# The second output projection of a two-layer encoder, begun for all row tiles in the last recurrent head

## The chip, the cores and the metric

The kernel runs on one NeuronCore of a Trainium2 chip. The time is device time in microseconds (us) of one execution. The kernel before takes 2702.19 us (median of three runs, 2701.62 to 2704.5).

The engines, by the names used below: TensorE (PE: matmuls; PEld: loads of the stationary operand, which overlap them), VectorE (DVE), ScalarE (ACT), GpSimd (POOL) and SyncE (SP), which here issues most DMAs. Each engine works through its own instructions in a fixed order.

## The reference, cut to what matters

Two layers over 1024 tokens of width 1024 (all float32). Layer 0 mixes tokens by windowed attention, layer 1 by a bidirectional gated recurrence (HGRN2) of 8 heads; each mixer also has 4 cross-attention heads of width 128 into 256 memory tokens. Both groups share one input and one output projection, and each layer ends with a convolutional feed-forward part.

```python
for layer in range(DEPTH):
    u = rmsnorm(h, norm_g[layer, 0])
    mem_kv = mem_n @ w_mem_kv[layer]
    if kind == 0:
        y = mixer_window_attn(u, mem_kv, ...)
    elif kind == 1:
        y = mixer_hgrn2(u, mem_kv, ...)
    h = h + rmsnorm(y, norm_g[layer, 1])
    f = conv_ffn(rmsnorm(h, norm_g[layer, 2]), ...)
    h = h + rmsnorm(f, norm_g[layer, 3])

def mixer_hgrn2(u, mem_kv, w_in, lb_fwd, lb_bwd, norm_g, w_out):
    q, i, zf, zb, gate, xq = jnp.split(u @ w_in, ...)
    ...
    o = gla_chunked(q, k_f, v, lf_f) + flip_t(gla_chunked(flip_t(q), flip_t(k_b), flip_t(v), flip_t(lf_b)))
    o = rmsnorm(o, ...) * jax.nn.silu(gate)
    return jnp.concatenate([o, memory_cross_attn(xq, mem_kv)], axis=-1) @ w_out
```

The last line is the output projection that the change is about: its input has 8 x 128 columns of recurrent heads and 4 x 128 of cross heads, 12 blocks of 128; its output has 1024 columns.

## The kernel before

*Precision.* Every float32 product of the projections is made of three matmuls (`mm3`, lines 80 to 83): each operand is split into a high part, a copy rounded to the type `float32r` (ScalarE), and a low part, the remainder (VectorE). `split` (line 85) does this for activations, `wunit` (line 69) for weights: it reads a unit of 128 x 1024 from DRAM into a staging buffer and writes a pair `wh`, `wl` into a ring of 4 pairs, or `xwh`, `xwl` into a pool that is handed to it.

*Tiles.* Tokens are cut into 8 row tiles of 128, or two blocks of 512 (b = 0, 1). The normalised rows `u` are kept transposed and split in `uh`, `ul`, of 8 blocks of 128 features by 1024 tokens.

*Order of work.* Pieces are written out in program order; a scheduler that works with a model of the engines turns this order into priorities and fixes each engine's order: an instruction further on is taken ahead where an engine would be free in the model and the instruction's inputs are there. `tc.high_priority` lifts single pieces. On the chip each engine follows the fixed order and waits on semaphores.

*The recurrence* (`hgrn`, from line 939). For each head, `proj` (line 1044) makes q, the two gates' inputs f and b (block by block, `proj_fm`), and for pairs of heads v and the output gate (`proj_tm`), in the order of the strings `ORD` (line 38); those of head h + 1 stand behind head h. For head 7 the order is `q0 f0 q1 b1`, and f1 and b0 only after its first and second direction. V and G (line 945) hold v and the gate of three heads in turn (slot h mod 3). `head` (line 1224) runs `direction` for (d, b) = (0,0), (1,1), (0,1), (1,0): a chain of VectorE, ScalarE and GpSimd operations (a scan at line 1091, products of decays, `ER` at line 1155), block products on TensorE (`pa`), transposes (line 1165) and state updates (`pu`, line 1170; `S`, line 1179). Then `output` (line 1182) runs for b = 1 and b = 0: products `po`, sums of squares, scaling, transposes, and `ot`, which goes by SP's queue to `oT[1][h]` in DRAM (line 1207). The products of the projections go through two PSUM banks `pj`.

*The cross units* (`cross_unit`, line 185) each make one block of one cross head: a query projection from `uh`, `ul`, scores, softmax, transposes, products, and `xo`, stored to `oT[1][8 + h]` by ScalarE's queue. `xo` shares its one buffer with `ot`. A new cross head first loads weights and its keys and values (`cross_head`, line 178), through an `E` buffer of the directions. `HX` (line 35) says how many units stand behind each of a head's four directions and two outputs: heads 2, 4, 6 have two (behind the third and fourth direction), head 7 has two (behind the second and third).

*The output projection of layer 1* (`WOut`, line 371; `wo1`). It runs over the two column halves of the weights, 12 blocks of 128 rows of weights in 6 units each, tiles in the order 4, 5, 6, 7, 0, 1, 2, 3. `early` (line 381), called behind head 7's third direction, begins tiles 4 and 5 in the two `pj` banks with heads 0 to 5 and cross heads 0 and 1. `open` (line 394), behind the fourth, adds the other two cross heads to these two. `finish` (line 465) makes the first half for all tiles: each group of blocks is read from `oT`, split (`operands`, `rows_of`), multiplied; heads 6 and 7 come last. It keeps the first half in `y0`. The second half reads and splits all 12 blocks again, per tile; then follow the norm, the residual and the next norm, whose transposed rows go into `uh`, `ul` (`norm_T`, line 107) for the feed-forward part, which begins on tiles 4 to 7.

Of the kernel before, what the change touches and what calls it, by code (L numbers as in the profile page):

```python
# [6 lines left out]
F32 = mybir.dt.float32  # L7
# [24 lines left out]
QKV_POOL = (0, 2, 2, 2)  # L32

XU = [(0, 2), (0, 2), (2, 2), (0, 0)]
HX = [(0,) * 6, (0,) * 6] + [(0, 0, 1, 1, 0, 0), (0,) * 6] * 2 + [(0, 0, 1, 1, 0, 0), (0, 1, 1, 0, 0, 0)]


ORD = ["QFB q0 f0 b0 q1 f1 b1 V v01234567"] + ["QFB q0 f0 q1 b1 f1 b0", "QFB q0 q1 f0 f1 b1 b0 V v01234567"] * 3 + ["QFB q0 f0 q1 b1|f1|b0"]
# [8 lines left out]
def build(tc, A, out):  # L47
# [32 lines left out]
    def mm3(o, ah, al, bh, bl, first, last):  # L80
        pe.matmul(o, ah, bh, start=first, stop=False)  # L81
        pe.matmul(o, ah, bl, start=False, stop=False)  # L82
        pe.matmul(o, al, bh, start=False, stop=last)  # L83

    def split(h, l, src):
        act.copy(h, src)  # L86
        dve.tensor_tensor(l, src, h.bitcast(F32), op=ALU.subtract)  # L87
# [283 lines left out]
    class WOut:  # L371
# [3 lines left out]
        def __init__(self, l, src, key, order):  # L375
            self.l, self.src, self.key, self.order = l, src, key, order
            self.pools = [[], [], []]
            self.pre, self.part, self.begun, self.us = {}, {}, {}, {}
            self.psb, self.tag, self.psb2 = None, "pb", None

        def early(self, psb, npre, es):

            self.psb, self.tag = psb, "pj"
            self.load(0, 4)
            for t in self.order[:npre]:
                self.pre[t] = self.bank()
                self.begun[t] = []
                for ks in (range(0, 4), range(4, 6), range(8, 10)):
                    oh, ol = [es.tile([P, 4, P], F32R, tag="s", bufs=5, name="oe")[:, :len(ks), :] for _ in range(2)]
                    raw = stg.tile([P, 1024], F32, tag="st", name="oraw")[:, :len(ks) * P].rearrange("p (k t) -> p k t", t=P)  # L390
                    self.rows_of(self.pre[t], t, ks, oh, ol, raw, not self.begun[t], False)
                    self.begun[t] += ks

        def open(self, npre, nsb):

            l = self.l
            self.w1 = tc.alloc_tile_pool(name=f"wa{l}", bufs=2, reuse_waits="tile")
            if self.psb is None:
                self.psb = tc.alloc_tile_pool(name=f"wopb{l}", bufs=npre, space=PSUM, reuse_waits="tile")
            self.pools = [[self.w1] for _ in range(3)]  # L400
            if l == 0:

                self.w1.tile([P, 512], F32, tag="part", bufs=nsb, name="part")
                for g in (0, 2):
                    self.operands(g)
                for _ in range(2):
                    for x in ("xwh", "xwl"):
                        self.w1.tile([P, 1024], F32R, tag=x, name=x)
                self.operands(1)
            self.load(0)  # L410
            if self.pre:
                for t in self.pre:
                    self.products(self.pre[t], t, 1, left=True)
                return
            for t in self.order[npre:npre + nsb]:
                ps = self.bank()
                self.products(ps, t, 0)
                self.products(ps, t, 1, True)
                self.part[t] = self.w1.tile([P, 512], F32, tag="part", bufs=nsb, name="part")
                act.copy(self.part[t], ps)  # L420
            for t in self.order[:npre]:
                self.pre[t] = self.bank()
                for g in range(2):
                    self.products(self.pre[t], t, g)

        def bank(self):
            if self.psb2:
                return self.psb2.tile([P, 512], F32, tag="pb2", name="pb")
            return self.psb.tile([P, 512], F32, tag=self.tag, name="pb")

        def load(self, b, n=6):
            for i, u in enumerate((0, 1, 2, 4, 5, 3)[:n]):
                if (b, u) not in self.us:
                    self.us[b, u] = wunit(A[self.key][b, u], pl=self.w1 if i >= RING else None)
            self.b = b
# [88 lines left out]

    def mmk(o, n, st, mv, first):
# [409 lines left out]
    def hgrn():  # L939
# [104 lines left out]
        def proj(h):  # L1044

            r = {"q": [None, None], "s": [[None, None], [None, None]], "v": V[:, h % 3], "gs": G[:, h % 3]}
            us = {}

            def load(w):
                if w not in us:  # L1050
                    us[w] = [wunit(A["wvg"][h // 2, u]) for u in range(4)] if w == "v" else wunit(A["wqz"][h, "qfb".index(w)])
                return us[w]

            def run(text):
                for x in text.split():
# [126 lines left out]
        def output(h, r, b, qin, S, As):  # L1182
            po = bank("po")
            ss = wp.tile([P, 4], F32, tag="oss", bufs=2, name="oss")
            for c in range(4):
                cg = 4 * b + c
                cs = slice(cg * P, (cg + 1) * P)
                ops = [(As[b][:, c, :], r["v"][:, cg, :])]
                if cg > 0:
                    ops.append((qin[0][:, cs], S[0][:, cg, :]))  # L1190
                if cg < NT - 1:
                    ops.append((qin[1][:, cs], S[1][:, cg, :]))
                for i, (x, y) in enumerate(ops):
                    pe.matmul(po[:, c, :], x, y, start=i == 0, stop=i == len(ops) - 1)  # L1194
            for c in range(4):
                sumsq(wp, po[:, c, :], ss[:, c:c + 1])
            rs = rstd_of(wp, ss, 4, P, "o")
            on = wp.tile([P, 4, P], F32, tag="on", bufs=1, name="on")
            for c in range(4):
                dve.scalar_tensor_tensor(on[:, c, :], po[:, c, :], rs[:, c:c + 1], r["gs"][:, 4 * b + c, :],  # L1200
                                         op0=ALU.mult, op1=ALU.mult)
            tp = bank("pt")
            for c in range(4):
                pe.transpose(tp[:, c, :], on[:, c, :], ident)
            ot = wp.tile([P, 512], F32, tag="ot", bufs=1, name="ot").rearrange("p (c t) -> p c t", c=4)
            act.activation(ot, tp, AF.Identity, scale=bng[:, h:h + 1])
            nc.sync.dma_start(oT[1][h, :, b * 512:(b + 1) * 512], ot.rearrange("p c t -> p (c t)"))

        units = [(h, b) for h in range(4) for b in ((1, 0) if h == 3 else (0, 1))]
        xhead = [None, None]  # L1210

        def cross(n):
# [11 lines left out]
        def head(h, r):  # L1224
            qin = [wp.tile([P, T], F32, tag=f"qin{d}", bufs=1, name="qin") for d in range(2)]
            S = [wp.tile([P, NT, P], F32, tag=f"S{d}", bufs=1, name="S") for d in range(2)]
            As = [None, None]
            for i, (d, b) in enumerate(((0, 0), (1, 1), (0, 1), (1, 0))):
                direction(h, r, d, b, qin[d], S[d], As)
                if i < len(r["later"]):  # L1230
                    r["run"](r["later"][i])
                cross(HX[h][i])
                if h == 7 and i == 2:
                    wo1.early(psj, 2, es)
            if h == 7:
                early.release()
                es.release()
                eq.release()
                wo1.open(2, 0)
            for i, b in enumerate((1, 0)):  # L1240
                output(h, r, b, qin, S, As)
                cross(HX[h][4 + i])

        cur = proj(0)
        for h in range(8):
            head(h, cur)
            if h < 7:
                cur = proj(h + 1)
        psp.release()
        wp.release()  # L1250
        late.release()


    def start():
# [26 lines left out]
        psp.release()  # L1281

    wo0 = WOut(0, A["x"], "wout0", list(range(NT)))
    wo1 = WOut(1, h2d, "wout1", [4, 5, 6, 7, 0, 1, 2, 3])
    start()
    window()
    wo0.finish()
    ffn(0, wo0, h2d, True, (0, 1), (0, 1))
    hgrn()
    wo1.finish()  # L1290
    ffn(1, wo1, out, False, (1, 0), (1, 0))
    for p_ in (up, ring, stg, cp, dram):
        p_.release()
# [81 lines left out]
```

## Time and profile before

| | |
|---|---|
| median of 3 runs | 2702.19 us (2701.62 to 2704.5) |
| profiled execution | 2705.6 us |
| its span, first to last instruction | 2703.8 us |
| mean granted clock of TensorE | 0.992 |
| share of the span: PE, PEld | 97%, 81% |
| DVE, ACT, POOL | 68%, 52%, 17% |
| instructions | 39480 |
| bytes moved by DMA | 432.25 MB |

The profile is of one execution, by the chip's own recorder. Its views: a page of totals; the chain of work that ended last, followed back from the last instruction (in the chain a piece's length is the time it alone held up the end); groups of instructions by line or tile; a table of stretches of time with each engine's busy time and the clock that TensorE was granted; the single instructions in order of time. A row of the last kind has start, length, engine, line, operation, output and inputs, shapes and a count, and in brackets how long the engine stood idle before it and who released it. Times count from the span's start. Matmuls overlap, so that the time from one start to the next is what one costs, and not its length.

### The profile page before, as it was taken

What the parts mean: (1) busy time and instruction counts of PE and PEld (TensorE: products, weight loads), DVE (VectorE), ACT (ScalarE), POOL (GpSimd) and SP (SyncE); (2) the same over time, 40 slices, a digit from 0 to 9 for tenths busy, and PEclk for the clock granted to TensorE, in tenths of its full rate; (3) what the DMA queues carried; (4) which work ended last, traced back from release to release, by engine and by line L of the source; (5) the groups of instructions that cost most, each with busy time, mean ns of one, the idle gap of its engine ahead of it and who ended that gap; (6) DMA issues with size and microseconds to landing.
All of it is one profiled execution on the core that took longest, in us unless ns stands there. A gap on an engine that the chain in (4) does not pass through costs nothing. (4 is left out here: it accounts for less than half of the span.)

```text
span 2703.8 us, 39480 instructions
## 1 busy us (share of the span) xinstructions
PE 2626.8 (97%) x14496; PEld 2202.5 (81%) x14496; DVE 1835.5 (68%) x3042; ACT 1397.5 (52%) x2556; POOL 469.3 (17%) x520
## 2 busy tenths in 40 slices
PE   8899999999999999999999999999899999999998
PEld 7888897788888887887888888888688788888887
DVE  6487787678555655478797796878467756556447
ACT  6367666645444444455554554545454444444443
POOL 1221110211111100032233231221021111110013
PEclk9899999999999999999999999999999999999999
DMA  7574213557878757574246331111466787774656
GB/s 282 206 165 105 59 31 117 180 186 176 215 192 208 199 158 245 195 244 153 83 140 158 79 91 51 56 48 45 136 206 178 180 216 200 204 202 158 224 192 232
DMA packets 215315, 432.25 MB, mean 160 GB/s; under 512 B 20560, under 2 KB 77264, under 8 KB 209488
## 3 DMA queue, kind: packets, MB, share of 16 engines
q1 hardware_dynamic: 188128, 335.07, 37.9%
q0 software_dynamic: 24544, 90.19, 16.0%
q10 hardware_dynamic: 2448, 4.46, 0.4%
q8 instruction: 114, 1.87, 0.3%
q14 instruction: 81, 0.66, 0.1%
HBM read 335.79 MB, written 117.96 MB: 168 GB/s over the span
## 5 line engine op out<-in xcount | busy, mean ns | idle before, releaser
L87 DVE TENSOR_TENSOR wl<-st,wh 128x1024 fp32r<-128x1024 f32 (+1 forms) x238 | 263.1, 1112 | 324.2 <-ACT wh L86 310.4
L86 ACT CAST wh<-st 128x1024 fp32r<-128x1024 f32 (+1 forms) x238 | 222.5, 937 | 294.6 <-PE X L535 193.1
L81 PE MATMUL pj<-uh,wh 128*128 128x512 f32 x512 | 204.2, 399 | 3.5 <-DVE xl L87 2.5
L535 PE MATMUL X<-wl,wh 128*128 128x512 f32 x528 | 204.8, 390 | 0.7 <-DVE wl L87 0.7
L535 PE MATMUL X<-wh,wl 128*128 128x512 f32 x528 | 204.6, 389 | 0.0
L82 PE MATMUL pj<-ul,wh 128*128 128x512 f32 x512 | 203.2, 397 | 0.1
L83 PE MATMUL pj<-uh,wl 128*128 128x512 f32 x512 | 202.3, 395 | 0.0
L535 PE MATMUL X<-wh 128*128 128x512 f32 x528 | 198.8, 390 | 2.9 <-ACT c L908 2.6
L81 PE MATMUL pj<-wh,uh 128*128 128x384 f32 (+1 forms) x512 | 190.7, 373 | 2.2 <-DVE gs L1022 2.2
L82 PE MATMUL pj<-wl,uh 128*128 128x384 f32 (+1 forms) x512 | 187.9, 367 | 0.0
L83 PE MATMUL pj<-wh,ul 128*128 128x384 f32 (+1 forms) x512 | 187.5, 367 | 0.0
L77 DVE TENSOR_TENSOR wl<-st,wh 128x1024 fp32r<-128x1024 f32 (+1 forms) x92 | 119.6, 1309 | 28.9 <-ACT wh L76 27.8
L535 PE MATMUL V<-uh,wh 128*128 128x512 f32 x344 | 133.8, 389 | 0.0
L535 PE MATMUL V<-ul,wh 128*128 128x512 f32 x344 | 133.8, 389 | 0.0
L535 PE MATMUL V<-uh,wl 128*128 128x512 f32 x344 | 133.8, 389 | 0.0
L76 ACT CAST wh<-st 128x1024 fp32r<-128x1024 f32 (+1 forms) x99 | 99.9, 1016 | 56.6 <-PE pj L82 34.8
L535 PEld LDWEIGHTS X<-wh 128*128 128x128 f32 x528 | 99.1, 188 | 24.3 <-ACT c L908 3.0
L535 PEld LDWEIGHTS X<-wl,wh 128*128 128x128 f32 x528 | 99.1, 188 | 21.6 <-DVE wl L87 1.3
L81 PEld LDWEIGHTS pj<-uh,wh 128*128 128x128 f32 x512 | 96.9, 189 | 24.3 <-DVE xl L87 2.9
L535 PEld LDWEIGHTS X<-wh,wl 128*128 128x128 f32 x528 | 99.1, 188 | 20.6
L83 PEld LDWEIGHTS pj<-uh,wl 128*128 128x128 f32 x512 | 97.0, 189 | 19.3
L82 PEld LDWEIGHTS pj<-ul,wh 128*128 128x128 f32 x512 | 97.0, 189 | 18.6 <-DVE ul L87 0.4
(347 smaller groups left out, 7227.2 us busy)
## 6 DMA issues: line engine op xcount, KB each, us to landing
st<-hid SPq DMA_DIRECT2D x154, 256.0 KB, 3.1
st<-in_ffw_dram SPq DMA_DIRECT2D x108, 256.0 KB, 3.2
w2s<-in_ffw_dram POOLq DMA_DIRECT2D x24, 1024.0 KB, 8.0
st<-in_ffw_dram SPq DMA_DIRECT2D x46, 512.0 KB, 4.1
hid<-tt SPq DMA_DIRECT2D x88, 256.0 KB, 4.6
st<-w2s SPq DMA_DIRECT2D x88, 256.0 KB, 2.8
sx<-in_ffw_dram SPq DMA_DIRECT2D x84, 256.0 KB, 3.9
sy<-in_ffw_dram SPq DMA_DIRECT2D x42, 512.0 KB, 6.4
```

The lines of the kernel that those rows point to most:

```text
L76: act.copy(h[:, :n], raw)
L77: (eng or dve).tensor_tensor(l[:, :n], raw, h[:, :n].bitcast(F32), op=ALU.subtract)
L81: pe.matmul(o, ah, bh, start=first, stop=False)
L82: pe.matmul(o, ah, bl, start=False, stop=False)
L83: pe.matmul(o, al, bh, start=False, stop=last)
L86: act.copy(h, src)
L87: dve.tensor_tensor(l, src, h.bitcast(F32), op=ALU.subtract)
L535: pe.matmul(o, x, y, start=new, stop=e, skip_group_check=not first)
```

## The change

A class `Out` takes the place of `WOut` for layer 1; layer 0 keeps `WOut`, without the early part.

- `HX`: the pairs of cross units stand in heads 0, 2, 4 and 6 (third and fourth direction); head 7 has none.
- Head 7's rows no longer go to DRAM: `output` writes them split into block 7 of `uh`, `ul`, scaling the transposes on ScalarE and subtracting on VectorE, both from PSUM.
- Behind head 7's second direction four units of the first half's weights are asked for, into the ring; `open`, where it stood, loads the other two (those of the cross heads) and sets out the buffers for the cross rows.
- `begin`, behind head 7's outputs in program order: for all 8 tiles the rows of heads 0 to 6 are read from `oT` into `ul`, split in place into `uh`, `ul` (free once head 7's projections are done), multiplied (21 matmuls a tile) in the two `pj` banks and copied to `y0`, which lies in slots 2 and 0 of V and G.
- `finish`, first half: the cross heads' four blocks are read and split, and multiplied together with block 7 in a new group of PSUM; VectorE adds the result to `y0`. Second half: blocks 0 to 7 from `uh`, `ul` as they lie, and the cross blocks read and split again. Norms and residual as before; `norm_T` writes over a tile's columns of `uh`, `ul` once they are used.
- V and G are released only after the projection, so the projection's buffers on that side lie elsewhere.

```diff
-HX = [(0,) * 6, (0,) * 6] + [(0, 0, 1, 1, 0, 0), (0,) * 6] * 2 + [(0, 0, 1, 1, 0, 0), (0, 1, 1, 0, 0, 0)]
+HX = [(0, 0, 1, 1, 0, 0), (0,) * 6] * 4
...
-        def early(self, psb, npre, es):
...
+    class Out:
+
+        def __init__(self, l, src, key, order):
...
+            n = (6, 7)[l]
+            self.groups = (range(0, n), range(8, 12), range(n, 8))
+            self.units = ((0, 1, 2, 4, 5, 3), (0, 1, 2, 3, 4, 5))[l]
...
+        def read(self, t):
+            k = self.groups[0]
+            c = (slice(None), slice(0, len(k)), slice(t * P, (t + 1) * P))
+            raw = ul[c].bitcast(F32)
+            nc.sync.dma_start(raw, oT[self.l][0:len(k), :, c[2]].rearrange("k p t -> p k t"))
+            act.copy(uh[c], raw)
+            dve.tensor_tensor(ul[c], raw, uh[c].bitcast(F32), op=ALU.subtract)
+
+        def kept(self, ps, t, ks, first, last):
+            for i, k in enumerate(ks):
+                m = slice(t * P, (t + 1) * P)
+                wh, wl = self.us[self.b, k // 2]
+                c = slice((k % 2) * 512, (k % 2 + 1) * 512)
+                mm3(ps, uh[:, k, m], ul[:, k, m], wh[:, c], wl[:, c], first and i == 0, last and i == len(ks) - 1)
+
+        def cross(self, ps, t, first, last):
+            ks = self.groups[1]
+            oh, ol = [self.ops.tile([P, 4, P], F32R, tag=x, bufs=n + self.l, name=x) for x, n in (("oh", 2), ("ol", 3))]
+            raw = ol.bitcast(F32)
+            self.last_read = nc.sync.dma_start(raw, oT[self.l][8:12, :, t * P:(t + 1) * P].rearrange("k p t -> p k t"))
+            split(oh, ol, raw)
...
+        def begin(self, psb, tag, n, y0):
+            self.psb, self.y0 = psb, y0
+            self.banks += [(psb, tag)] * n
+            for t in self.order:
+                if t in self.order[:2 - 2 * self.l]:
...
+                else:
+                    self.read(t)
+                ps = self.bank()
+                self.kept(ps, t, self.groups[0], True, True)
+                act.copy(y0[t], ps)
+            self.used = 0
+
+        def open(self):
+            self.w1 = tc.alloc_tile_pool(name=f"wa{self.l}", bufs=2, reuse_waits="tile")
+            self.ops = self.w1
+            self.load(0, self.w1)
...
+        def finish(self):
...
+            for t in self.order:
+                ps = self.bank()
+                self.cross(ps, t, True, False)
+                self.kept(ps, t, self.groups[2], False, True)
...
+                dve.tensor_tensor(y0[t], ps, y0[t], op=ALU.add)
+                sumsq(wp, y0[t], s0[:, t:t + 1])
...
+            self.load(1, self.w1)
...
+            for t in self.order:
...
+                self.kept(ps, t, range(8), True, False)
+                self.cross(ps, t, False, True)
...
+            if h == 7:
+                tp = tp.rearrange("p c t -> p (c t)")
+                oh, ol = (x[:, 7, b * 512:(b + 1) * 512] for x in (uh, ul))
+                act.activation(oh, tp, AF.Identity, scale=bng[:, h:h + 1])
+                dve.scalar_tensor_tensor(ol, tp, bng[:, h:h + 1], oh.bitcast(F32), op0=ALU.mult, op1=ALU.subtract)
+                return
...
-        units = [(h, b) for h in range(4) for b in ((1, 0) if h == 3 else (0, 1))]
+        units = [(h, b) for h in range(4) for b in range(2)]
...
-                if h == 7 and i == 2:
-                    wo1.early(psj, 2, es)
+                if h == 7 and i == 1:
+                    wo1.load(0, n=RING)
             if h == 7:
                 early.release()
                 es.release()
                 eq.release()
-                wo1.open(2, 0)
+                wo1.open()
...
+        free = [x[:, i].rearrange("p a b -> p (a b)") for i in (2, 0) for x in (V, G)]
+        wo1.begin(psj, "pj", 2, {t: free[i // 2][:, (i % 2) * 512:(i % 2 + 1) * 512] for i, t in enumerate(wo1.order)})
         psp.release()
         wp.release()
-        late.release()
+        return late
...
-    wo1 = WOut(1, h2d, "wout1", [4, 5, 6, 7, 0, 1, 2, 3])
+    wo1 = Out(1, h2d, "wout1", [4, 5, 6, 7, 0, 1, 2, 3])
...
-    hgrn()
+    late = hgrn()
     wo1.finish()
+    late.release()
```

More of the change, by code (lines that the diff above doesn't have):

```diff
@@ L379, in __init__ @@
             self.psb, self.tag, self.psb2 = None, "pb", None
-        def early(self, psb, npre, es):
[L383 to L392, printed above, removed]
         def open(self, npre, nsb):
@@ L410, in open @@
             self.load(0)
[L411 to L414, printed above, removed]
             for t in self.order[npre:npre + nsb]:
```

59 lines of the change are left out of this document (added).

## The prediction

> **What bounds the kernel now.** I read the page first, for its engines.
>
> ```profile
> PE 2626.8 (97%) x14496; PEld 2202.5 (81%) x14496; DVE 1835.5 (68%) x3042; ACT 1397.5 (52%) x2556; POOL 469.3 (17%) x520
> ```
>
> TensorE (PE) is busy 97% of the span. No edit here takes a matmul away, so the change is worth what it does to the holes in PE's work and to PE's clock. The table of stages says where these are (columns: length, then busy us and count of PE, weight loads, VectorE, ScalarE and GpSimd, then granted clock, DMA share, GB/s).
>
> ```profile
> 1300.00:1400.00 100.00, 99.68 (x800) 84.05 (x800) 80.84 (x154) 55.79 (x115) 28.34 (x31) 1.00 0.31 106
> 1829.00:1865.00 36.00, 36.00 (x258) 30.97 (x257) 30.38 (x66) 22.60 (x55) 7.00 (x8) 1.00 0.08 27
> 1865.00:1880.00 15.00, 15.00 (x139) 12.65 (x138) 13.29 (x22) 10.15 (x20) 2.80 (x4) 1.00 0.24 80
> 1880.00:1932.00 52.00, 38.44 (x311) 29.94 (x310) 34.04 (x77) 22.55 (x61) 9.96 (x11) 0.90 0.36 114
> 1932.00:1976.00 44.00, 44.00 (x191) 36.27 (x191) 12.66 (x21) 17.73 (x36) 8.47 (x6) 0.97 0.51 153
> 1976.00:2058.00 82.00, 81.10 (x387) 67.48 (x386) 60.13 (x96) 45.38 (x84) 10.60 (x16) 1.00 0.61 200
> ```
>
> Head 7 runs from 1829. Its last 52 us hold 52 - 38.44 = 13.56 us of idle PE at a clock of 0.90. The projection behind it is dense but for 82 - 81.10 = 0.90 us at its end. Time lost to the low clock, as busy time times what the clock lacks: 38.44 x 0.10 + 44 x 0.03 = 5.2 us. So 13.56 + 0.90 + 5.2 = 19.7 us are lost from 1829 to 2058, and that is all this change can play for. The chain in order of time (start, length, what) names the holes.
>
> ```profile
> 1870.43 2.22 DMA oT<-ot
> ...
> 1905.57 1.57 ACT xp L208 x7
> ...
> 1913.12 3.60 DMA or<-oT
> ...
> 1917.52 5.05 DMA or<-oT
> ...
> 2605.09 27.89 PE V L535 x123
> ```
>
> Two things end waits there: the softmax of a cross unit (ScalarE's `xp`, 1905) whose transposes stand in PE's queue ahead of head 7's own work, and reads of `oT`, the heads' rows in DRAM, one after another (from 1913 on). The last row gives a price: 123 back-to-back matmuls of 512 columns in 27.89 us, 0.2268 us each.
>
> **The change part by part.**
>
> *Work moved, not removed.* Each row tile needs 12 x 3 matmuls per column half before and after: 8 x 2 x 36 = 576. That sums to nought.
>
> *The cross units.* Two leave head 7; one pair each now stands in heads 0, 2, 4 and 6. Two more prices from the chain, a unit's transposes and the products of a head's output:
>
> ```profile
> 1848.38 0.44 PE pt L217 x4
> ...
> 1857.01 1.79 PE po L1194 x16
> ```
>
> One unit is 24 + 6 matmuls of 512 columns (30 x 0.2268 = 6.8 us), 12 of 256 (half of 0.2268 each: 1.4) and 8 transposes at 0.11 (0.9): 9.1 us. Two are 18.2 us of PE. Head 0 has no hole to take them: 1300 to 1400 is busy 99.68 of 100. So head 7 starts about 18 us later, and its own stretch has 18 us less to do: nought again, but cover leaves head 7. With a unit go its weight load and conversion (ScalarE, VectorE), its read of keys and values on SP's queue and its store on ScalarE's; they pass into queues that have room in head 0 (VectorE 80.84, ScalarE 55.79 of 100). I put that at 0, bounds -1 and +2 us.
>
> *The early start and `begin`.* The early part (two tiles, 48 matmuls, 10.9 us) goes; `begin` brings 8 x 21 = 168 matmuls, 38.1 us of cover, of which none needs head 7's own rows. Cover in head 7 thus goes from 29 to 38 us. It can start only once head 6's rows have gone to DRAM and come back, and this is the dear step. Its rows, of before (d0 = 1829.36, the start of head 7's first direction):
>
> ```profile
> 1829.36 0.63 ACT L1084 ACTIVATE E<-s 128x512 f32<-128x512 f32 x1 [3.33 <-DVE s L1041]
> 1865.08 0.33 ACTq L224 DMA_DIRECT2D oT<-xo  x1
> 1865.18 0.69 DVE L1041 TENSOR_SCALAR s<-pj 128x512 f32<-128x512 f32 x1
> 1868.49 0.63 ACT L1084 ACTIVATE E<-s 128x512 f32<-128x512 f32 x1 [2.57 <-DVE kvl L87]
> 1869.74 0.67 ACT L1206 ACTIVATE ot<-pt,bng 128x512 f32<-128x512 f32 x1
> 1914.55 1.05 ACT L76 CAST xwh<-st 128x1024 fp32r<-128x1024 f32 x1
> 1916.73 0.83 ACT L86 CAST oh<-or 128x768 fp32r<-128x768 f32 x1 [0.34 <-DMA or<-oT]
> 1917.65 0.96 DVE L87 TENSOR_TENSOR ol<-or,oh 128x768 fp32r<-128x768 f32 x1
> 1944.91 0.58 ACT L485 COPY y<-pb 128x512 f32<-128x512 f32 x1
> ```
>
> The last projection that reads the normalised rows is taken from PSUM at 1865.18, d0 + 35.8. What PE then had of projections was the two cross units' queries, and they leave:
>
> ```profile
> 1865.00:1878.00 13.00, 10.44 (x43) 1.00 0.27 92
> ```
>
> (PE time on `pj` alone.) Of these 13 us, which PE filled, only 13 - 10.44 = 2.6 us stay, about one direction's share. Head 6's upper block is written from 1869.74 and lands at 1870.43 + 2.22 = 1872.65; then comes the read for `begin`, 448 KB. The 384 KB read before the ScalarE row of 1916.73 took the 3.60 us of the chain's row at 1913.12; I take 3.8. One row of the DMA view (KB, median us to landing) is wanted beside it:
>
> ```profile
> oT<-xo ACTq DMA_DIRECT2D x16, 256.0 KB, 2.6
> ```
>
> With these 3.8 us and the copy to `uh` (896 columns, between 0.83 and 1.05: 0.95) the first matmul stands at 1872.65 + 3.8 + 0.95 = 1877.4, d0 + 48.0. The hole is 48.0 - 35.8 - 2.6 = 9.6 us. The write at 1869.74 had waited behind `kvl` and, through a buffer it shares with `xo`, behind the store of 1865.08 (2.6 us to land: 1867.7); with no cross unit in head 7 the first wait goes, so up to 2 us come back. I take **8 us**; ends: 4 (the whole cross unit of head 6 done 4 us sooner, as ScalarE and VectorE carry less) and 16 (a read of 5.05 that queues behind another store, split later in line).
>
> *The low clock behind the hole.* In before:
>
> ```profile
> 1889.39 0.47 PE L81 MATMUL pb<-wh,oe 128*128 128x512 f32 x1 [1.66 <-DVE nm L205]
> 1891.09 0.80 PE L83 MATMUL pb<-wh,oe 128*128 128x512 f32 x1 [0.99 <-DVE oe L87]
> 1891.68 0.63 PE L81 MATMUL pb<-wh,oe 128*128 128x512 f32 x1
> 1892.11 0.63 PE L82 MATMUL pb<-wl,oe 128*128 128x512 f32 x1
> 1931.62 0.79 PE L81 MATMUL pb<-xwh,oh 128*128 128x512 f32 x1 [3.93 <-ACT oh L86]
> 1934.34 0.89 PE L1204 MATMUL pt<-ident,on 128*128 128x128 f32 x4
> ```
>
> After 3.93 us of idle, six matmuls took 1934.34 - 1931.62 = 2.72 instead of 1.36 us; after pieces of 1.66 and 0.99 us the spacing was 0.43 too. One to two such restarts: **2 us**, ends 1 and 4. The Trainium skill (TensorE: Matmul & The Clock Gate, "What's actually happening") has the clock halved only after an idle window of about 3.4 us; the short matmuls of a direction would break this hole into shorter pieces, so by that rule this term would be 0 and the sum below 2 us lower. The rows above, slow after two pieces well under 3.4 us, speak against counting on it.
>
> *Supply of `begin` after its first tile.* A tile feeds PE for 21 x 0.2268 = 4.8 us and asks 0.95 + 0.58 = 1.5 us of ScalarE and about 1.05 of VectorE; its read has its own place in `ul`, so all eight can be in flight; behind their eight issues on SP's queue there stand only the weights of units 4 and 5 and the reads of the first half, wanted 40 us later. Two PSUM banks alternate. VectorE is the tight one: 13.29 of 15 us between 1865 and 1880, of which a cross split, an early split and weights' splits are to go. **2 us**, ends 0 and 8.
>
> *Head 7's tail.* Its last direction ended its chain on VectorE at 1902.55 (next row), d0 + 73.2; without the cross units' share of VectorE and their `E` buffer I expect d0 + 64: the second direction, bound by PE's projections, starts as before relative to d0, and the two behind it take 14 us each (1868.49 to the same operation at 1882.55). From 1902.55 to the last transposes of the output (1934.34 + 0.89) went 32.7 us, with the softmax and the reads in the way; even that long again is d0 + 97. `begin`, two directions and two outputs (22 products at 0.112 and 4 transposes at 0.11 each: 2.9 us) keep PE till 48.0 + 38.1 + 5.2 + 5.8 + 2, about d0 + 99. So the tail, the direct write of head 7's rows (no trip through DRAM; one VectorE operation of 0.7 us in its place) and the lost cross cover cost nothing, with 2 to 14 us to spare.
>
> ```profile
> 1881.87 0.68 DVE L1155 TENSOR_TENSOR ER<-ER,s 128x512 f32<-128x512 f32 x1
> ...
> 1901.87 0.68 DVE L1155 TENSOR_TENSOR ER<-ER,s 128x512 f32<-128x512 f32 x1
> ```
>
> *Second half.* It rereads 4 instead of 12 blocks per tile and splits a third as much. PE was dense there, so 0; the 0.90 us at the end stay.
>
> **Sum.** Lost after: 8 + 2 + 2 + 0.9 = 12.9 us; before 19.7; gain 6.8 us, or 0.25%. The profiled execution (span 2703.8, 2705.6 with what lies around it) would be 2697.0 in span; the median shown, 2702.19, is 3.4 below that execution, and gives **2695.4 us**. The ends of the terms give losses of 5.9 to 28.9, with -1 and +2 for head 0: 2687 to 2713.
>
> **The rivals.** *The hole takes the gain back.* If `begin`'s first matmul comes at d0 + 54 (read and split each wait their turn), the hole is near 15 us and the losses, 15 + 2 + 2 + 0.9 = 19.9, equal those of before: 2702, taken as 2697 to 2707. For it: the write and its read are in line behind one another on SP's queue. Against it: nothing else reads DRAM much there (DMA share 0.24).
>
> *Slower: the splits queue behind the directions.* VectorE and ScalarE run in the order written; `begin` is traced after head 7's outputs, so its splits may stand behind the third and fourth direction. If the first is past d0 + 64, the hole is 64 + 1.5 - 35.8 less 2.6, two more directions' 5.2 and an output's 2.9: 19.0 us, with 3 + 2 + 0.9 a loss of 24.9, 5.2 more than before: 2707; each further us of delay adds nearly one, and I take the case as 2707 to 2716. It decides from about d0 + 54 on. For it: VectorE's 13.29 of 15 us. Against it: those 13.29 us hold splits of a cross unit and of the early start, which go.
>
> *A larger gain.* The early landing (hole 4), no stall of supply: loss 6 to 8, 2688 to 2691. For it: the kv buffer's wait goes. Against it: four steps in a row each at their best.
>
> **How the numbers follow.** Forecast (2692 to 2699) 0.43; hole takes it back 0.21; slower 0.23; larger gain 0.13. The bound for a difference is 0.2%, 5.4 us: 2696.8 and 2707.6. Three quarters of the forecast's case and all of the larger gain lie below the first: 0.46. The rest of the forecast and most of the second case lie within: 0.29. The slower case and a little of the second: 0.25. The range 2686 to 2711 leaves out the far half of the slower case and a trace of the larger gain.
>
> **What the profile after would show.** Holes of PE by stage: 6 to 10 us between head 7's last projection and the first `kept` matmul, ended by ScalarE's copy into `uh`; near none from there to the second half; no read of `oT` on the chain after head 7; spacing 0.43 after the hole for 2 to 4 us. Head 7's first direction near 1847; its last chain on VectorE some 9 us earlier relative to it. Wrong would be: a first `kept` matmul later than d0 + 54; evictions into the dead `V` and `G` room that wait for head 7's last reads, so that PE stops after two tiles; new holes in head 0 over 2 us; a stall where the second half's weights load.

## The result, and the profile after

The changed kernel takes 2697.98 us (median of 20 runs), the kernel before 2702.43 us beside it (20 runs): a ratio of 0.9980, with a 95% interval of 0.9974 to 0.9987. By the medians it is 4.4 us, 0.16%, faster, by the ratio some 5.4 us, 0.20%. Forecast were 2695.4 us and a gain of 6.8 us. The profiled execution after took 2697.36 us (span 2695.5), 0.6 below that median; the one before, 2705.6, stood 3.2 above its own. So the two traces lie 8.3 us apart where the medians lie 4.4 apart. Of the 8.3 us, 1.6 lie ahead of layer 1, in work that the change does not touch: the last transposes of its input rows start at 1259.94 before and at 1258.33 after, with 5973 matmuls up to there in both.

The page's totals of the kernel after:

```profile
PE 2622.5 (97%) x14496; PEld 2202.1 (82%) x14496; DVE 1831.1 (68%) x3024; ACT 1385.1 (51%) x2528; POOL 468.2 (17%) x520
```

The count of matmuls is the same, 14496; 18 operations of VectorE and 28 of ScalarE have gone. The table of stages of the kernel after, with the columns of before. Head 7's first direction now starts at 1849.31 (first row of the fence after this one), and I call this moment d0 again.

```profile
1269.00:1849.00 580.00, 568.16 (x4509) 478.35 (x4508) 444.97 (x874) 298.66 (x646) 149.00 (x162) 1.00 0.31 88
...
1849.00:1885.00 36.00, 36.00 (x311) 30.68 (x312) 30.36 (x66) 22.78 (x55) 6.99 (x8) 1.00 0.12 37
1885.00:1900.00 15.00, 7.00 (x102) 5.42 (x96) 13.61 (x25) 9.79 (x17) 2.93 (x4) 0.80 0.67 193
1900.00:1937.00 37.00, 36.67 (x257) 31.21 (x257) 27.64 (x47) 19.15 (x41) 10.01 (x9) 0.99 0.40 115
1937.00:1970.00 33.00, 33.00 (x149) 27.34 (x148) 11.58 (x18) 10.98 (x22) 6.10 (x5) 1.00 0.46 150
1970.00:2051.00 81.00, 79.63 (x381) 66.30 (x380) 52.61 (x83) 34.73 (x68) 14.17 (x18) 1.00 0.40 140
```

All the idle time of TensorE in head 7 is now one hole of 15 - 7.00 = 8.0 us between 1885 and 1900. From 1900 to the end of the projection it stands still for 0.33 and 1.37 us. Its rows, in order of time (start, length, engine, operation; idle time before it and who ended it):

```profile
1849.31 0.63 ACT L1188 ACTIVATE E<-s 128x512 f32<-128x512 f32 x1 [3.33 <-DVE s L1145]
...
1885.15 0.69 DVE L1145 TENSOR_SCALAR s<-pj 128x512 f32<-128x512 f32 x1
...
1889.72 0.66 PE L1269 MATMUL pt<-ident,ER 128*128 128x128 f32 x4 [4.08 <-ACT ot L1316]
...
1891.05 2.07 PE L1274 MATMUL pu<-v,kT 128*128 128x128 f32 x8 [0.68 <-ACT kT L1271]
...
1897.22 0.54 PE L81 MATMUL pb<-wh,uh 128*128 128x512 f32 x1 [3.25 <-ACT uh L537]
...
1944.48 0.75 DVE L1313 SCALAR_TENSOR_TENSOR ul<-pt,bng,uh 128x512 fp32r<-128x512 f32 x1 [4.53 <-ACT uh L1312]
...
2049.12 1.06 PE L116 MATMUL pt<-ident,nu 128*128 128x128 f32 x8 [1.37 <-DVE nu L112]
```

The last projection leaves PSUM at d0 + 35.8, and the first matmul of `begin` (`pb` from `wh`, `uh`) stands at d0 + 47.9. Between them the two directions in reach break the hole into 4.08, 0.68 and 3.25 us. The chain of waits of the kernel after, through the hole (start, length, what):

```profile
1885.84 1.96 DVE wl L77
1887.80 0.65 DVE Az L1260
...
1888.46 0.62 ACT As L1264
1889.08 0.60 ACT ot L1316
...
1889.69 2.55 DMA oT<-ot
...
1892.31 3.90 DMA ul<-oT
...
1896.23 0.95 ACT uh L537
```

Read it from the end. `begin` waits for its split (0.95), that for the read (3.90), that for the landing of head 6's last rows (2.55), and these for `ot`, which ScalarE could make only behind work of head 7's direction (`As`), itself behind the low part of a weight (`wl`, 2 us on VectorE). Of the 11.4 us from 1885.84 to the first matmul at 1897.22, 6.5 are the trip through DRAM.

### The profile page after: what moved, and what is told of

It is laid out like the page before. It is cut to its first block, busy times and chain, and to the rows that moved or that the text cites. A ratio compares the mean times of both kernels' runs of the same rounds, so it can differ in the third digit from the quotient of the medians.

```text
span 2695.5 us, 39322 instructions
## 1 busy us (share of the span) xinstructions
PE 2622.5 (97%) x14496; PEld 2202.1 (82%) x14496; DVE 1831.1 (68%) x3024; ACT 1385.1 (51%) x2528; POOL 468.2 (17%) x520
## 4 chain that ended last, share of the span: by engine, by line
PE 76%; DVE 13%; ACT 4%; DMA 4%; issue 2%; POOL 1%; SPq 0%; DVEq 0%; POOLq 0%; ACTq 0%
PE X L639 26%; PE V L639 11%; PE pj L81 5%; PE pj L82 5%; PE Y L639 5%; PE pj L83 5%; PE pb L82 3%; PE pb L81 3%; PE pb L83 3%; DVE E L1195 1%; DVE ER L1230 1%; DVE wl L77 1%; PE pt L338 1%; DVE wl L87 1%; PE pt L116 1%
```

## The experiments

The edits are to the kernel after, but for the first, and each computes the whole reference. A kernel's ratio is to the kernel before on the same chip. The kernel after stands at 0.9980 (0.9974 to 0.9987) on this scale.

### The cross units alone

To the kernel before, this one part of the change:

```diff
-HX = [(0,) * 6, (0,) * 6] + [(0, 0, 1, 1, 0, 0), (0,) * 6] * 2 + [(0, 0, 1, 1, 0, 0), (0, 1, 1, 0, 0, 0)]
+HX = [(0, 0, 1, 1, 0, 0), (0,) * 6] * 4
...
-        units = [(h, b) for h in range(4) for b in ((1, 0) if h == 3 else (0, 1))]
+        units = [(h, b) for h in range(4) for b in range(2)]
```

> The kernel before with one edit: the cross units stand in heads 0, 2, 4 and 6, as in the changed kernel; the early start of two tiles, the trip of head 7's rows through DRAM and the rest of the projection stay. Theory (begin's cover for all tiles makes the gain): head 7 loses 18 us of cover and has 11 us of early matmuls left, so PE idles more there: 5 to 15 us slower than before. Rival (the gain is that no softmax stands in PE's queue at the end of head 7): 3 to 8 us faster than before. A second use: holes of PE from the first head to head 7, which were 2.7 us more in the changed kernel, should be 2 to 4 us more here too if the units' new places make them.

Measured: 2705.87 against 2702.88 us, 1.0009 (1.0000 to 1.0018), 3 us slower or nothing. The stages ahead of head 7 and at its end:

```profile
1271.00:1851.00 580.00, 568.83 (x4515) 479.20 (x4514) 445.71 (x874) 299.55 (x648) 148.97 (x162) 1.00 0.31 88
1885.00:1940.00 55.00, 41.38 (x379) 32.78 (x378) 39.87 (x81) 25.68 (x60) 13.63 (x16) 0.91 0.41 127
```

Neither the theory (5 to 15 us slower) nor the rival (3 to 8 us faster) came true. With the softmax out of the way, head 7's last 55 us still hold 13.6 us of idle TensorE, as many as before. What the softmax's leaving may give and what the lost cover takes are not told apart here; the two together gain nothing. And the 580 us ahead of head 7 hold 11.2 us of idle.

### The cross units back in head 7

```diff
-HX = [(0, 0, 1, 1, 0, 0), (0,) * 6] * 4
+HX = [(0,) * 6, (0,) * 6] + [(0, 0, 1, 1, 0, 0), (0,) * 6] * 2 + [(0, 0, 1, 1, 0, 0), (0, 1, 1, 0, 0, 0)]
...
-        units = [(h, b) for h in range(4) for b in range(2)]
+        units = [(h, b) for h in range(4) for b in ((1, 0) if h == 3 else (0, 1))]
```

> The changed kernel with the cross units placed as before (two in head 7, behind its second and third direction); all else as changed. Theory: the hole of 8 us between head 7's last projection and the first kept matmul is filled by the two units' queries (10.4 us), and begin covers the units' softmax: 4 to 8 us faster than the changed kernel, 8 to 14 faster than before. Rival (the gain is that the softmax left PE's queue in head 7): as slow as before, within 2 us, or slower. A third way: the units read the normalised rows until d0 + 48, so begin is late by what the units bring, and the time is that of the changed kernel within 2 us.

Measured: 0.9976 (0.9965 to 0.9987), which the interval doesn't part from the kernel after: the 4 to 8 us of the theory did not come, and the time is that of the third way. Stages ahead of head 7 and from its start on:

```profile
1270.00:1826.00 556.00, 547.76 (x4403) 461.40 (x4403) 433.48 (x844) 286.83 (x616) 150.43 (x162) 1.00 0.31 89
1826.00:2027.00 201.00, 192.58 (x1184) 159.96 (x1183) 130.20 (x238) 95.89 (x206) 37.26 (x40) 0.98 0.35 113
```

Ahead of head 7 the idle time falls from 580 - 568.16 = 11.8 to 556 - 547.76 = 8.2 us: the units' new places cost some 3 us there. Behind it the units cover part of the hole and bring waits of their own (201 - 192.58 = 8.4 us of idle, where the kernel after has 9.7), so little is won.

### Head 6 read apart

```diff
         def read(self, t):
-            k = self.groups[0]
-            c = (slice(None), slice(0, len(k)), slice(t * P, (t + 1) * P))
...
+            for ks in (slice(0, 6), slice(6, 7)):
+                c = (slice(None), ks, slice(t * P, (t + 1) * P))
```

(Read and split are done twice per tile: six heads that lie in DRAM long before, and head 6 alone.)

> The changed kernel with the rows of head 6 read and split apart from those of heads 0 to 5 (two reads and two pairs of split operations a tile in begin, in place of one), so that 18 of a tile's 21 matmuls need no wait for head 6's trip through DRAM. Theory: the first kept matmul comes 5 to 7 us earlier after head 7's last projection, the hole of 8 us shrinks to 1 to 4, and the time is 3 to 7 us below the changed kernel. Rival (the hole is covered by slack elsewhere, or the splits on VectorE and ScalarE set begin's start): the same time within 1.5 us.

Measured: 2691.41 us, 0.9960 (0.9947 to 0.9972), 5 us below the kernel after. The stage of the hole and what is left in it:

```profile
1885.00:1900.00 15.00, 12.29 (x123) 9.45 (x123) 14.79 (x30) 11.40 (x27) 2.74 (x3) 1.00 0.49 156
```

```profile
1881.60 0.40 PE L81 MATMUL pb<-wh,uh 128*128 128x512 f32 x1
...
1891.32 0.66 PE L1269 MATMUL pt<-ident,ER 128*128 128x128 f32 x4 [0.31 <-ACT ot L1316]
...
1894.12 0.66 PE L1269 MATMUL pt<-ident,ER 128*128 128x128 f32 x4 [0.99 <-ACT ot L1316]
...
1895.92 0.50 PE L81 MATMUL pb<-wh,uh 128*128 128x512 f32 x1 [0.17 <-ACT uh L537]
...
1898.83 1.13 PE L1274 MATMUL pu<-v,kT 128*128 128x128 f32 x8 [1.25 <-ACT uh L537]
```

2.7 us of idle instead of 8.0, and the clock is whole. `begin` now has its first matmul at 1881.60, 33.6 us behind the start of head 7's first direction (1847.96 here), where it had stood at d0 + 47.9: the rows of six heads do not wait for those of head 6, and 18 of a tile's 21 matmuls can run ahead of them. The wait of all seven for head 6's rows is what most of the hole was made of.

### Head 7's rows through DRAM

```diff
-            if h == 7:
...
-                act.activation(oh, tp, AF.Identity, scale=bng[:, h:h + 1])
-                dve.scalar_tensor_tensor(ol, tp, bng[:, h:h + 1], oh.bitcast(F32), op0=ALU.mult, op1=ALU.subtract)
-                return
...
+                self.read(t, slice(7, 8))
```

(The read stands in the first half, ahead of block 7's products.)

> The changed kernel with head 7's rows written to DRAM as the other heads' are, and read and split into block 7 of the kept rows in the first half, tile by tile. Theory (the direct write is off the path, since begin's matmuls cover head 7's tail): within 2 us of the changed kernel. Rival (the direct write makes the gain): 4 to 10 us slower than the changed kernel, a hole of PE ended by the copy of block 7.

Measured: 0.9980 (0.9971 to 0.9989), the same as the kernel after. The stage from `begin` to 3 us short of the projection's end:

```profile
1900.00:2048.00 148.00, 148.00 (x815) 124.47 (x810) 90.41 (x150) 65.28 (x133) 30.34 (x32) 0.99 0.44 143
```

TensorE isn't idle in it at all, so the trip through DRAM is hidden. The direct write is worth nothing here.

### Four tiles, and two, in `begin`

```diff
-            for t in self.order:
+            for t in self.order[:4]:
...
+                late = t in self.order[4:]
+                if late:
+                    self.read(t)
...
+                if late:
+                    self.kept(ps, t, self.groups[0], False, False)
```

(The other tiles get their 21 matmuls in the first half, in the same group of PSUM as the rest, and ScalarE copies them to `y0`; the second run has 2 in place of 4.)

> The changed kernel with begin for four of the eight row tiles (4 to 7); the rows of the other four are read, split and multiplied in the first half of the projection, behind head 7. Theory (begin's matmuls are the cover that makes the gain): cover falls from 38 to 19 us, PE runs dry some 30 us after its first kept matmul and idles till head 7's last output: 8 to 20 us of new holes before the first half, less what head 7's tail gains from a freer VectorE: 5 to 14 us slower than the changed kernel. Rival (four tiles are enough cover, the rest of begin only shifts work): within 2 us of the changed kernel.

> The changed kernel with begin for two row tiles (4 and 5); the other six are read, split and multiplied in the first half. With four tiles the time stayed that of the changed kernel, since the first half's cross products ran in the two PSUM banks before head 7 ended and only one hole of 2.3 us was new. Theory (cover is enough as long as begin's and these products last till head 7's outputs): with two tiles cover ends some 10 us earlier, new holes of 6 to 12 us appear before head 7's last output, 3 to 10 us slower than the changed kernel. Rival (head 7's tail shortens by what begin leaves to VectorE and ScalarE): within 2 us of the changed kernel.

Measured: four tiles 0.9983 (0.9974 to 0.9991), the same as eight, as the rival had it; two tiles 1.0023 (1.0015 to 1.0032), some 11 us slower than eight. The stage of four tiles, and rows that say what filled it:

```profile
1885.00:1945.00 60.00, 50.96 (x362) 42.60 (x363) 44.29 (x81) 31.01 (x64) 17.26 (x15) 0.86 0.53 160
```

```profile
1926.11 0.39 PE L81 MATMUL pb<-xwh,oh 128*128 128x512 f32 x1
...
1938.27 1.16 PE L1316 MATMUL pt<-ident,on 128*128 128x128 f32 x4 [2.25 <-DVE on L1312]
```

At 1926.11 the first half's own products (`pb` from `xwh`, `oh`: the cross heads) already run, 12 us ahead of head 7's output transposes at 1938.27. I had counted as cover only what `begin` brings; the first half brings its own. With two tiles it no longer reaches:

```profile
1890.00:1945.00 55.00, 41.70 (x302) 34.66 (x303) 40.01 (x77) 27.66 (x58) 14.29 (x12) 0.76 0.56 160
```

```profile
1899.69 0.80 PE L81 MATMUL pb<-wh,uh 128*128 128x512 f32 x1 [3.74 <-ACT uh L537]
...
1919.92 1.22 PE L1306 MATMUL po<-S,qin 128*128 128x128 f32 x4 [3.23 <-DVE S L1291]
...
1929.25 0.78 PE L81 MATMUL pb<-xwh,oh 128*128 128x512 f32 x1 [1.51 <-ACT oh L86]
```

There are 13.3 us of idle, and the clock of 0.76 takes 41.70 x 0.24 = 10 us more.

### Rows read again for the second half

```diff
             for t in self.order:
...
+                self.read(t)
                 self.kept(ps, t, range(8), True, False)
```

> The changed kernel, but the second half reads and splits the rows of heads 0 to 6 again for every tile, so that nothing is saved by keeping them. Theory (the second half is bound by PE and the saved reads and splits were off the path): within 2 us of the changed kernel. Rival (keeping the rows is part of the gain): 3 us or more slower.

Measured: 0.9980 (0.9971 to 0.9988), the same as the kernel after. The second half, up to its last 6 us:

```profile
1985.00:2050.00 65.00, 65.00 (x313) 54.34 (x312) 41.81 (x71) 26.28 (x52) 8.90 (x14) 1.00 0.42 144
```

TensorE is dense with the reads and splits in. Keeping the rows split from `begin` to the second half gains no time.

### Another place for the cross heads' `xo`

`ot` shares its buffer with `xo`, and must wait until the store of `xo` has read it. Two runs give `xo` of layer 1 another buffer. In the first it is a staging buffer of the weights:

```diff
-        ot = w0.tile([P, 512], F32, tag=tags.get("xo", "xo"), bufs=1, name="xo")
+        if l == 1:
+            ot = stg.tile([P, 1024], F32, tag="st", name="xo")[:, :512]
+        else:
+            ot = w0.tile([P, 512], F32, tag="xo", bufs=1, name="xo")
```

In the second it is the softmax rows' own buffer:

```diff
-        ot = w0.tile([P, 512], F32, tag=tags.get("xo", "xo"), bufs=1, name="xo")
+        if l == 1:
+            ot = w0.tile([P, 4, 256], F32, tag="sm", bufs=1, name="xo")[:, :2, :].rearrange("p a b -> p (a b)")
```

> The changed kernel with the cross units' result in a staging buffer, so that head 6's output buffer has no cross store to wait for. Theory (the shared buffer is one of the steps that make the hole): head 6's upper block lands 1 to 3 us earlier and the hole shrinks from 8 to 5 to 7 us: 1 to 3 us faster than the changed kernel. Rival (ScalarE's queue, where the output stands behind operations of a direction, holds it anyhow): the same within 1 us; the staging buffer might also delay a weight load by as much.

> The changed kernel with the cross units' result of layer 1 in the buffer of their softmax rows, which are dead by then, so that head 6's output has no cross store to wait for and no staging buffer is taken. Theory (the shared buffer is a step of the hole): the hole of 8 us ends 1 to 3 us earlier, 1 to 3 us faster than the changed kernel. Rival (ScalarE's queue holds head 6's output, behind a copy that waits for a mask operation of VectorE, which stands behind a weight split): same hole, within 1.5 us of the changed kernel. The next unit's softmax now waits for the store; it is a direction later.

Measured: the first 2772.76 us, 1.0245 (1.0232 to 1.0258). Its stage ahead of head 7 has 610 - 568.83 = 41 us of idle, spread over the heads, so it says nothing of the hole. Which transfer the staging buffer held up I did not trace.

```profile
1270.00:1880.00 610.00, 568.83 (x4380) 468.25 (x4380) 432.79 (x846) 287.60 (x621) 148.75 (x161) 0.96 0.27 77
```

The second: 2697.05 us, 0.9970 (0.9959 to 0.9981), whose interval overlaps that of the kernel after. Its rows at head 7's start and in the hole, and then its waits of TensorE ahead of head 7 (us in total, times, longest):

```profile
1855.57 0.63 ACT L1191 ACTIVATE E<-s 128x512 f32<-128x512 f32 x1 [1.86 <-DVE s L1148]
...
1884.25 0.69 ACT L1319 ACTIVATE ot<-pt,bng 128x512 f32<-128x512 f32 x1
...
1891.31 0.30 PE L1311 MATMUL pt<-ident,on 128*128 128x128 f32 x1 [0.39 <-DVE on L1307]
...
1894.76 0.65 PE L81 MATMUL pb<-wh,uh 128*128 128x512 f32 x1 [1.85 <-ACT uh L540]
```

```profile
PE pj L81 <- DVE gs L1129: 7.2, 5, 3.9
PE pt L1311 <- DVE on L1307: 3.5, 1, 3.5
```

```profile
1270.00:1855.00 585.00, 571.46 (x4505) 481.49 (x4504) 443.42 (x873) 296.36 (x644) 149.66 (x162) 0.99 0.31 87
```

`ot` is made at d0 + 28.7 instead of d0 + 39.8 (1889.08 in the chain above), and the hole is 2.2 us instead of 8.0: the shared buffer is one of the hole's steps. But d0 itself, the start of head 7, comes 6.3 us later, and most of the gain goes there; on the span's own clock `ot` is 4.8 us earlier. Idle time ahead of head 7 grew by only 585 - 571.46 - 11.84 = 1.7 us, for other waits became shorter (those for GpSimd's `E` fell from 4.8 to 1.2 us). The rest is busy time, 571.46 us instead of 568.16 for about as many matmuls: behind the two long waits shown, of 3.9 and 3.5 us, the clock was 0.56 from 1454.89 to 1458.50 and 0.54 from 1621.60 to 1625.00, which is some 3 us. What makes these waits longer I did not find out.

### One cross unit in head 7

```diff
-HX = [(0, 0, 1, 1, 0, 0), (0,) * 6] * 4
+HX = [(0,) * 6] * 2 + [(0, 0, 1, 1, 0, 0), (0,) * 6] * 2 + [(0, 1, 1, 1, 0, 0), (0, 1, 0, 0, 0, 0)]
...
-        units = [(h, b) for h in range(4) for b in range(2)]
+        units = [(h, b) for h in range(4) for b in ((1, 0) if h == 3 else (0, 1))]
```

Three runs go with this: the places alone, the places with head 6 read apart, and, beside them, head 6 read apart with two units in head 7 as before.

> The changed kernel with the cross units in heads 2 and 4 (two each), head 6 (three) and head 7 (one), head 6's rows read as in the changed kernel. Theory: the 3.5 us lost ahead of head 7 come back, and the one unit in head 7 fills part of the hole of 8 us with its query's 5.4 us: 5 to 9 us faster than the changed kernel, and at most 4 us above the run that has these places and head 6 apart. Rival (only the apart reading of head 6 made that run fast): 2 to 4 us faster than the changed kernel.

> Head 6's rows read and split apart; of the eight cross units two stand in heads 2 and 4, three in head 6 and one in head 7, behind its second direction; none in head 0. Theory: the 3.5 us that the units cost in head 0 come back, and with one unit, done early in head 7, no softmax stands late in PE's queue: 2 to 4 us below the run with head 6 apart alone. Rival (a unit in head 7 delays begin or the tail by as much): the same as that run within 1.5 us, or slower.

> Head 6's rows read and split apart, and the cross units placed as before (two in head 7). Theory: the units' dearer new place costs 3.5 us (holes ahead of head 7 that the run with only the units moved had too) and is undone here, but the units' queries already fill the hole that the apart reading fills; what stays is the units' softmax at the end of head 7 (some 4 us of holes after 1930 in the run with the units back): between the two single edits' times, 2690 to 2696. Rival (both gains add up): 2684 to 2688.

Measured: the places alone 0.9973 (0.9960 to 0.9986), not parted from the kernel after, and not the 5 to 9 us of the theory; with head 6 read apart 2690.39 against 2706.49 us, **0.9943 (0.9931 to 0.9955)**, the fastest of all; with two units in head 7 0.9967 (0.9956 to 0.9978), between the two single edits (0.9976 and 0.9960) as its theory had it. With the places alone the hole stays:

```profile
1889.36 0.77 PE L1269 MATMUL pt<-ident,ER 128*128 128x128 f32 x4 [4.37 <-ACT ot L1316]
```

With one unit in head 7 and head 6 read apart the stage of the hole has 1.3 us of idle, and from 1834 to the projection's end there are 2.7 us:

```profile
1880.00:1900.00 20.00, 18.68 (x155) 14.82 (x155) 19.27 (x41) 14.52 (x27) 5.78 (x7) 1.00 0.60 191
1834.00:2043.00 209.00, 206.32 (x1278) 173.46 (x1278) 145.78 (x272) 106.12 (x232) 44.75 (x44) 1.00 0.39 124
```

This version is below both the kernel before and the kernel after. Against head 6 read apart alone (0.9947 to 0.9972) the intervals overlap, so the single unit's own worth is suggested, not shown. And the reason given for it, that the 3.5 us lost ahead of head 7 come back, did not hold:

```profile
1269.00:1834.00 565.00, 552.99 (x4412) 464.16 (x4411) 433.50 (x845) 290.14 (x622) 148.41 (x162) 1.00 0.32 88
```

```profile
1790.13 0.47 PE L81 MATMUL pj<-wh,uh 128*128 128x512 f32 x1 [2.07 <-DVE gs L1126]
```

There are 12.0 us of idle ahead of head 7 as in the kernel after (11.8). The wait of 1.26 us for `gs` that the kernel after has behind the units of head 0 (at 1471.92) is gone, but both runs with three units in head 6 have a new one of 2.07 us (here at 1790.13).

## Why the prediction was right, point by point

- *What can be played for.* Of the 19.7 us lost from head 7 on, there remain 8.0 (hole) + 0.3 + 1.4 of idle, and at a low clock 7.00 x 0.20 + 36.67 x 0.01 = 1.8 us: 11.5, where 12.9 were forecast. That part of the gain is 8.2 us.
- *The hole of 8 us, first matmul near d0 + 48.* 8.0 us and d0 + 47.9. The steps came in the order written: the last projection out at d0 + 35.8 again, a write of 2.55, a read of 3.90 (3.8 taken), a split of 0.95. That the size was hit is partly luck. The working gave 9.6 us, and 1.6 were taken off because `ot` would no longer wait for `kvl`. It did not, but it now waited for `As` and `wl` and came at d0 + 39.8 (1889.08) where it had come at d0 + 40.4, so the first matmul came no earlier than worked out. What made the hole smaller is that 47.9 - 35.8 - 8.0 = 4.1 us of other work lay in it and not 2.6, a part of it slowed by the low clock.
- *The cross units at 0, bounds -1 and +2.* This is the term that was mis-sized, and it lies outside its bounds. Ahead of head 7 idle time grew from 558 - 548.85 = 9.15 us (the first fence below, of before) to 11.84, by 2.7 us; with the units as before it is 8.2. The other traces agree: counted from the transposes that open the layer to d0, idle time is 11.2 to 12.6 us in the seven traces with the units moved as here and `xo` in its old buffer (the kernel after, the units alone, head 6 apart, head 7 through DRAM, four tiles, two tiles, rows read again), and 8.8 to 9.2 us in the three with the units as before (the kernel before, the units back, and these with head 6 apart). The waits of TensorE over these stretches, before and then after, say where it went:

```profile
1271.00:1829.00 558.00, 548.85 (x4407) 461.94 (x4406) 434.82 (x848) 288.84 (x619) 151.88 (x162) 1.00 0.31 89
```

```profile
PE pj L81 <- DVE gs L1022: 2.2, 4, 0.8
...
PE pj L81 <- DVE q L1036: 0.2, 1, 0.2
```

```profile
PE pj L81 <- DVE gs L1126: 3.9, 5, 1.3
PE pj L81 <- DVE q L1140: 1.5, 2, 1.1
```

  The projections wait for VectorE to empty their PSUM banks (`gs`, `q`), 5.4 instead of 2.4 us; with the units alone moved they make 5.1 us, with the units moved back 2.2. I had looked at the room in 100 us of head 0, as a mean, and not at what a projection waits for. With it the gain is 8.2 - 2.7 = 5.5 us; the medians show 4.4, the ratio 5.4. That the total came this near has luck in it: a good part of what the units cost too much was made up by the supply of `begin`, 1.7 us better than taken.
- *Low clock, 2 us.* 1.8 in this trace. With nearly the same hole three other traces lose more: over 15 us of it the clock was 0.64 (head 7 through DRAM), 0.58 (four tiles) and 0.69 (rows read again), a loss of 2.4 to 3.4 us. The Trainium skill's rule (TensorE: Matmul & The Clock Gate, "What's actually happening"), a halved clock only after an idle window of some 3.4 us, gave 0 here, because I took the hole to be in shorter pieces; two of its pieces turned out to be 4.08 and 3.25 us, so this hole does not decide against the rule. The run with the units alone speaks against it, as the last section shows.
- *Supply of `begin`, 2 us.* 0.3 us: all eight tiles came in time. *The end of the second half, 0.9:* 1.4.
- *Head 7's tail, at 0, ending by d0 + 97.* Its last rows were written at 1944.48 to 1945.23, d0 + 95.9, with TensorE busy. That the end fits is luck: VectorE ended the last direction's chain at d0 + 70.3 (1919.58), only 2.9 us earlier than before and not at d0 + 64, and the way from there to the last rows took 25.7 us and not 32.7. The price of 14 us for a direction had also been misread: its two times, 1868.49 and 1882.55, are the first ScalarE operation of a direction and the end of the `ER` product, not the same operation twice. The direct write at 0 held (head 7 through DRAM: same time), and so did the second half at 0 (rows read again: same time).
- *Cover of 29 to 38 us.* The sign was right and the need was overstated: the first half's cross products run ahead of head 7's end, so four tiles are enough, and two are not.
- *The rivals.* The splits did not queue behind the directions (the first at d0 + 46.9, far from d0 + 64), and the hole did not reach 15 us. The larger gain did not come by itself. Two edits took most of the hole away, another buffer for `xo` and a read apart, but only the second came near that time (0.9960).

What stays open: why VectorE empties the banks later with the units moved ahead, when its own load there is not full, and why the same waits grow once more with `xo` in the softmax rows' buffer.

## What to carry to other kernels

Where a projection begins early to fill a hole, ask which of its inputs comes last, and read that one apart from those that have lain ready for long: here one read for seven heads made six wait for the seventh, and parting it took 5.3 of 8.0 us from the hole. Count as cover everything that needs nothing from the late part, also what lies further on in the order, before paying for more. Work that is moved to an earlier stage is to be priced by what that stage's own waits would do, not by the mean room of its engines.

## What the runs showed of the hardware

TensorE's granted clock stayed at 1.00 in a stage of 15 us with 2.7 us of idle in pieces of at most 1.25 us (head 6 read apart), and fell to 0.80 in the same stage with pieces of 4.08, 0.68 and 3.25 us (the kernel after). With 13.3 us of idle in 55 us, in pieces of at most 3.74 us behind one of 4.08, it was 0.76 over the whole stage (two tiles). In that case the clock cost 10 us beside the 13.3 of idle; in the kernel after 1.8 beside 8.0; with short pieces nothing.

The length of a piece alone does not decide. In the run with the units alone TensorE was busy from 1851.00 to 1887.90 without a break, then stood still once, for 2.96 us (3.35 us from the start of the last matmul ahead), and 1.06 us after it had begun again ran at half its clock for 3.41 us (row, then stage):

```profile
1890.93 0.51 PE L83 MATMUL pb<-wh,oe 128*128 128x512 f32 x1 [2.96 <-DVE oe L87]
```

```profile
1891.99:1895.40 3.41, 3.41 (x10) 2.54 (x9) 2.77 (x5) 1.49 (x4) 0.00 (x0) 0.50 0.35 117
```

In the kernel before, 3.93 us of idle were followed by 3.37 us at a clock of 0.51 (1931.62 to 1934.99), but 3.03 us of idle shortly before by 3.37 us at 1.00 (1923.13 to 1926.50). The Trainium skill's window of about 3.4 us (same page and section), taken as the least idle time that halves the clock, is therefore not borne out: 2.96 us were enough once, and so were, in the kernel before, two pieces of 1.66 and 0.99 us with 0.7 us of work between them and TensorE busy without a break ahead of them from 1829.00 to 1887.70. What decides in between stays open.
